# A hybrid trunk layer: triangular inverse on POOL, token shift without copies, key norms by logarithm, undecayed states, pooling beside the last group's fills through DRAM

## The chip, the cores and the metric

The kernel runs on one core of a Trainium2 chip. Its time is the device time of one execution in microseconds (us), as the median of several runs. All times below are from the kernel before the change unless a sentence says otherwise.

## What is computed

One layer of a streaming trunk for 256 prompt tokens and 64 sample tokens (320 together), with a model width of 2048, all in 32-bit floats:

```
h = RMSNorm(x);  [u_pool | u_rwkv | g_pool | g_rwkv] = h @ w_in
A: pooling mixer on u_pool: trailing means over 2/4/8/16 tokens minus the token, a linear map per group, a scale
B: RWKV-7 on u_rwkv: token shift, low-rank decay / rate / gate, 16 heads x 64,
   S = S * w_t + (S @ -kk) b_t + v_t k_t;  y = S @ r   (kk has norm 1), group norm, bonus
x += (sigmoid(g_pool) * (A @ proj_pool) + sigmoid(g_rwkv) * (B @ proj_rwkv)) @ w_out
x += SwiGLU(RMSNorm(x));  x += sigmoid(RMSNorm(x) @ w_ple_gate) * (p @ w_ple_proj);  final RMSNorm
```

Outputs are y and the new shift, pooling and wkv states.

## The kernel before

**Matmuls.** Every weight matrix streams from HBM in units of eight 128x128 blocks (`unit`): SP loads `raw`, ACT rounds it to `wh` (line 98), DVE takes the rest `wl = raw - wh` (`TT`, line 56), three buffers each. PE then does three matmuls of 320 columns per block (`mm3`, lines 115 to 117): `wh*xh`, `wh*xl`, `wl*xh`. A gemm with 16 blocks of depth has two units and 48 matmuls. The cast `wl_f0_8` is that of the fill tile f0 from block 8 on.

**The recurrence.** The 16 heads are worked on in four groups of four heads (`group`). A group takes six projected tiles (`acc_q...`), shifts them by one token (`shift`), and makes decay factors (`cum`, `p5`, `pcs`, `pinv`), the normalised keys (`rsqrt_tp`) and the operands `ar` and `bk` of five chunks of 64 tokens. Their products (PE, `g0` and `g4`) are masked on DVE into `mg`. Each 64x64 chunk matrix needs a triangular inverse. Its diagonal 32x32 blocks, 40 in a group, go through DRAM (`dF`, written and read by POOL's DMA queue) into a tile `xb` with one block on each of 40 partitions. 30 steps invert them there, each a multiplication into `tm` and an addition into `xb`, so 60 operations of 30 to 240 elements per partition. One `tensor_scalar` adds 1 on the diagonal; DMAs through `dX` and `dT` bring the blocks back, and PE makes the off-diagonal block (`pz`, `px`). Then four steps over the chunks (`ra`, `pu`, `ps_s`, `py_c`) carry the state `sbd`: new state = (`ps_s` + old state) times the decay `pcs`.

**Work between.** Behind group g stand `FILLS[g]` tiles of independent gemms (`acc_f`, 40 in all: 8 for `u_pool`, 32 for the gates), whose results go to DRAM. After the last group the pooling mixer (`pool_load`, `pool_diff`, `pool_mix`) reads `d_u` back, makes the differences on DVE, multiplies them by the pool weights (`acc_pw`), and the remaining five fills follow. Then come the projections, the feed-forward part and the last gate.

**Order.** A scheduler sets each engine's order from the program and its dependencies when the program is built; priorities (`tc.high_priority`) pull weight units ahead. Each engine runs its queue in order, and an instruction that waits holds back everything behind it. DVE and POOL have one such queue each; POOL's also issues its DMAs.

Of the kernel before, what the change touches and what calls it, by code (L numbers as in the profile page):

```python
# [48 lines left out]
def trunk_step(ctx: ExitStack, tc: tile.TileContext, xT, pT, cols, w_low, s0T, poolpast, cst, maskc, invc,  # L49
# [103 lines left out]
    def col(c, n=1):  # L153
        return ct[:, c:c + n]
# [3 lines left out]

    def shift(q, rp, t, out):

        pool.tensor_copy(out=rp[:, 0:5:4, 0], in_=ssz[:, q, :])
        pool.tensor_copy(out=rp[:, 1:4, 0], in_=rp[:, 0:3, C])
        pool.tensor_copy(out=nshift[:, q, :], in_=rp[:, 3:5, C])
        act.activation(t, rp[:, :, 1:], AF.Copy, scale=omu[:, q:q + 1])
        stt(out.rearrange("p (c t) -> p c t", c=NCH), rp[:, :, 0:C], col(C_MU + q), t, ALU.mult, ALU.add)


    fill_q = list(range(-8, 32))
# [20 lines left out]
    with tc.tile_pool(name="start", bufs=1) as st:  # L189
# [97 lines left out]
                        pe.matmul(out=acc[0:n], lhsT=w, rhs=x, start=k == 0 and n == P, stop=k == KD - 1 and n == P)  # L287

        def low(q, a=None):
            rp = st.tile([P, NCH, C + 1], F32, tag="rp", name="rp0", bufs=2)  # L290
            xs = xstd.rearrange("p (c t) -> p c t", c=NCH)
            if a is None:
                a = small(f"acc_t{q}", [P, NT], ("", "s", "cs")[q])
                if q == 2:
                    narrow(a, w_in[q])
                else:
                    gemm(a, w_in[q], KD, f"t{q}", xs_in)
            ac = a.rearrange("p (c t) -> p c t", c=NCH)
            if q == 2:
                r3 = st.tile([P, NT], F32, tag="xm0", name="r3", bufs=2)  # L300
                for i in range(3):
                    act.copy(r3[32 * i:32 * i + 32], a[96:128])
                TT(rp[0:96, :, 1:], ac[0:96], r3[0:96].rearrange("p (c t) -> p c t", c=NCH), ALU.add)
                mul(rp[0:96, :, 1:], rp[0:96, :, 1:], xs[0:96])
                mul(rp[96:128, :, 1:], ac[96:128], xs[96:128])
            else:
                mul(rp[:, :, 1:], ac, xs)
            t = st.tile([P, NCH, C], F32, tag="tsh", name="tsh0", bufs=2)
# [41 lines left out]
    def pool_diff(gi, z):  # L350

        pool.dma_start(out=o_pool[:, 0, 2 * gi:2 * gi + 2, :], in_=z[:, :, T_P:T_P + PAST])
        pool.dma_start(out=o_pool[:, 1, 2 * gi:2 * gi + 2, :], in_=z[:, :, ZL - PAST:])
        cur, w = z, 1
        while w < WINS[gi]:
            s = rf.tile([P, 2, ZL], F32, tag="tp", name="s", bufs=6)
            lo = 2 * w - 1
            TT(s[:, :, lo:], cur[:, :, lo:], cur[:, :, lo - w:ZL - w], ALU.add)
            cur, w = s, 2 * w
        d = rf.tile([P, 2, NT], F32, tag="tp", name="d", bufs=6)  # L360
        inv = 1.0 / WINS[gi]
        a, b = PAST, 2 * PAST + T_P
        t16 = rk.tile([P, 2, 16], F32, tag="tm", name="t16")
        mul(t16, cur[:, :, a:a + 16], iv[:, gi:gi + 1, :].broadcast_to([P, 2, 16]))
        TT(d[:, :, 0:16], t16, z[:, :, a:a + 16], ALU.subtract)
        stt(d[:, :, 16:T_P], cur[:, :, a + 16:a + T_P], inv, z[:, :, a + 16:a + T_P], ALU.mult, ALU.subtract)
        stt(d[:, :, T_P:], cur[:, :, b:], inv, z[:, :, b:], ALU.mult, ALU.subtract)
        dh = rf.tile([P, 2, NT], F32R, tag="tp", name="dh", bufs=6)
        act.copy(dh, d)
        dl = rf.tile([P, 2, NT], F32R, tag="tp", name="dl", bufs=6)  # L370
        TT(dl, d, f(dh), ALU.subtract)
        return dh, dl

    def pool_mix(gi, dh, dl):
        h, l = unit(w_poolw[gi], 4, f"pw{gi}")
        for i in range(2):
            j = 2 * gi + i
            a = small("acc_pw", [P, NT])
            mm3(a, [h[:, (2 * i + q) * P:(2 * i + q + 1) * P] for q in range(2)],
                [l[:, (2 * i + q) * P:(2 * i + q + 1) * P] for q in range(2)],  # L380
                [(dh[:, q, :], dl[:, q, :]) for q in range(2)], True, True)
            act.activation(yah[:, j, :], a, AF.Copy, scale=col(C_PS + j))
            stt(yal[j], a, col(C_PS + j), f(yah[:, j, :]), ALU.mult, ALU.subtract)

    def gate_tile(i):
        gt = sp.tile([P, NT], F32, tag="gate", name="gate", bufs=2)
# [6 lines left out]
    with tc.tile_pool(name="rk", bufs=1) as rk:  # L393

        def shift_tile(q, out):

            a = acc_tile(f"acc_q{q}")
            gemm(a, w_in[q], KD, f"q{q}", xs_in)
            rp = rf.tile([P, NCH, C + 1], F32, tag="rp", name="rp", bufs=3)
            mul(rp[:, :, 1:], a.rearrange("p (c t) -> p c t", c=NCH), xstd.rearrange("p (c t) -> p c t", c=NCH))  # L400
            t = rf.tile([P, NCH, C], F32, tag="tsh", name="tsh", bufs=2)
            shift(q, rp, t, out)

        W2 = [P, 2, NT]
# [1 line left out]
        def tp(name):  # L406
            return rf.tile(W2, F32, tag="tp", name=name, bufs=6)
# [15 lines left out]
        def group(g):  # L423
# [141 lines left out]
            for s in range(1, 31):  # L565
                n = 31 - s
                tm = rk.tile([40, s, n], F32, tag="tm", name="tm")
                mul(tm, xb[:, 0:s, s:s + 1].broadcast_to([40, s, n]), xb[:, s:s + 1, s + 1:32].broadcast_to([40, s, n]))
                TT(xb[:, 0:s, s + 1:32], xb[:, 0:s, s + 1:32], tm, ALU.add)
            diag = xb.rearrange("u s t -> u (s t)")[:, 0:1024:33]  # L570
            vec.tensor_scalar(out=diag, in0=diag, scalar1=1.0, scalar2=None, op0=ALU.add)
            act.copy(xbt, xb[0:20].rearrange("u s t -> u t s"))
# [30 lines left out]
            sbd_in = rk.tile([P, 2, P], F32, tag="sbd", name="sbd_in", bufs=4)  # L603
            pool.memset(sbd_in, 0.0)
            for h in range(2):
                pool.dma_start(out=sbd_in[64 * h:64 * h + 64, :, 64 * h:64 * h + 64],
# [11 lines left out]
                                  rhs=uv[:, c, 2 * jj + h, :], start=cur is None and h == 0, stop=h == 1)  # L618

            states = {4: sbd_in, 0: None}  # L620
            for cs in ((4, 0), (1,), (2,), (3,)):
                n = len(cs)
                ra = small("ra", [P, n, 2, C], "cs")
# [19 lines left out]
                                      rhs=uv[:, c, 2 * jj + h, :], start=True, stop=True)  # L643
                new = {}
                for i, c in enumerate(cs):
                    nxt = rk.tile([P, 2, P], F32, tag="sbd", name="sbd", bufs=4)
                    pool.memset(nxt, 0.0)
                    for lo in halves:
                        src = ps[lo, i]
# [65 lines left out]
        pool.dma_start(out=o_shift, in_=nshift)
        part = ap.tile([P, KD, NT], F32, tag="ah", name="part")
# [231 lines left out]
```

## Time and profile before

| | |
|---|---|
| median of 3 runs | 1900.65 us (1900.62 to 1900.97) |
| profiled execution | 1900.61 us, of which span 1898.7 us |
| busy: PE, DVE, ACT, POOL | 98%, 59%, 42%, 7% of the span |
| chain that ended last | PE 95%, DVE 3%, DMA 1%, issue 1% |
| mean granted TensorE clock | 0.993 |

The profiled execution is 1.9 us longer than its span, which runs from the first to the last instruction. In rows of the profile the engines are PE (matmul), DVE (vector), ACT (scalar), POOL (GpSimd) and SP (which issues weight loads); a row names its engine, its line of the kernel, its operation, `out<-in` by tile names, and the shape.

### The profile page before, as it was taken

To read this page: it belongs to the slowest core of one execution; us is meant where nothing else is said; L and a number is where in the kernel's file an instruction comes from. 1 tells how busy PE (TensorE), PEld (TensorE's weight loads), DVE (VectorE), ACT (ScalarE), POOL (GpSimd) and SP (SyncE) were. 2 spreads that over 40 slices of the span, in tenths; PEclk is the share of its full clock that TensorE was granted. 3 is DMA by queue.
4 is the path that set the end of the run, shared out by engine and by line. 5 is a ranking of instruction groups with operands and counts; after the bars stand their busy time and mean duration, and the time that the engine had idled before them with its cause. 6 is when DMAs were issued, how large, how long until landed. Compare 5 with 4: busy or idle time off the path is not lost.

```text
span 1898.7 us, 32757 instructions
## 1 busy us (share of the span) xinstructions
PE 1863.8 (98%) x13444; PEld 1838.0 (97%) x13444; DVE 1120.1 (59%) x1674; ACT 798.6 (42%) x1060; POOL 138.7 (7%) x282
## 2 busy tenths in 40 slices
PE   8999999899999999999999999999999999999997
PEld 7999999799989999999999999999999999999997
DVE  7676976877857465555454554444545554445655
ACT  6554536464455334443333333223333333333543
POOL 0110222202310112000000000000000000000000
PEclk9999999899999999999999999999999999999998
DMA  7554544345545657444444444554444444555553
GB/s 274 168 170 150 167 147 148 105 161 181 169 138 189 199 191 233 146 152 148 151 150 149 152 147 148 146 151 156 153 146 154 146 154 143 152 146 150 169 170 117
DMA packets 95349, 302.99 MB, mean 160 GB/s; under 512 B 12224, under 2 KB 23248, under 8 KB 95200
## 3 DMA queue, kind: packets, MB, share of 16 engines
q1 hardware_dynamic: 78336, 271.71, 44.3%
q0 software_dynamic: 6816, 17.39, 3.0%
q10 hardware_dynamic: 10048, 11.80, 1.7%
q8 instruction: 106, 1.74, 0.4%
q14 instruction: 43, 0.35, 0.1%
HBM read 284.12 MB, written 16.73 MB: 158 GB/s over the span
## 4 chain that ended last, share of the span: by engine, by line
PE 95%; DVE 3%; DMA 1%; issue 1%; ACT 0%; SPq 0%; DVEq 0%; ACTq 0%
PE acc_fd L115 5%; PE acc_fu L116 5%; PE acc_fg L116 5%; PE acc_fg L115 5%; PE acc_fg L117 5%; PE acc_fu L117 5%; PE acc_fd L116 5%; PE acc_fu L115 5%; PE acc_fd L117 5%; PE acc_f L115 4%; PE acc_f L116 4%; PE acc_f L117 4%; PE acc_q L117 3%; PE acc_q L115 3%; PE acc_q L116 3%; PE acc_pg L115 2%
## 5 line engine op out<-in xcount | busy, mean ns | idle before, releaser
L116 PE MATMUL acc_fg<-nl,wh_fg 128*128 128x320 f32 x704 | 217.8, 309 | 0.0
L115 PE MATMUL acc_fg<-nh,wh_fg 128*128 128x320 f32 x704 | 217.6, 309 | 0.1
L115 PE MATMUL acc_fu<-nh,wh_fu 128*128 128x320 f32 x704 | 217.5, 309 | 0.0
L117 PE MATMUL acc_fu<-nh,wl_fu 128*128 128x320 f32 x704 | 217.5, 309 | 0.0
L116 PE MATMUL acc_fu<-nl,wh_fu 128*128 128x320 f32 x704 | 217.5, 309 | 0.0
L117 PE MATMUL acc_fg<-nh,wl_fg 128*128 128x320 f32 x704 | 217.5, 309 | 0.0
L56 DVE TENSOR_TENSOR wl_fd<-raw_fd,wh_fd 128x1024 fp32r<-128x1024 f32 (+1 forms) x96 | 109.1, 1136 | 151.7 <-ACT wh_fd L98 151.7
L98 ACT CAST wh_fd<-raw_fd 128x1024 fp32r<-128x1024 f32 (+1 forms) x96 | 94.1, 980 | 203.1 <-PE acc_fd L116 162.4
L98 ACT CAST wh_fg<-raw_fg 128x1024 fp32r<-128x1024 f32 x88 | 92.5, 1051 | 199.1 <-PE acc_fg L116 98.7
L98 ACT CAST wh_fu<-raw_fu 128x1024 fp32r<-128x1024 f32 x88 | 92.5, 1052 | 190.8 <-PE acc_fu L116 103.4
L56 DVE TENSOR_TENSOR wl_fg<-raw_fg,wh_fg 128x1024 fp32r<-128x1024 f32 x88 | 107.8, 1225 | 105.3 <-ACT wh_fg L98 105.3
L115 PE MATMUL acc_f<-xh,wh_f 128*128 128x320 f32 x512 | 160.8, 314 | 1.7 <-ACT wh_f L98 1.7
L116 PE MATMUL acc_f<-xl,wh_f 128*128 128x320 f32 x512 | 160.6, 314 | 0.0
L117 PE MATMUL acc_f<-xh,wl_f 128*128 128x320 f32 x512 | 159.5, 312 | 0.8 <-DVE wl_f L56 0.8
L115 PE MATMUL acc_fd<-hh,wh_fd 128*128 128x320 f32 x512 | 158.2, 309 | 0.0
L116 PE MATMUL acc_fd<-hl,wh_fd 128*128 128x320 f32 x512 | 158.2, 309 | 0.0
L117 PE MATMUL acc_fd<-hh,wl_fd 128*128 128x320 f32 x512 | 158.2, 309 | 0.0
L56 DVE TENSOR_TENSOR wl_fu<-raw_fu,wh_fu 128x1024 fp32r<-128x1024 f32 x88 | 107.8, 1226 | 83.9 <-ACT wh_fu L98 83.9
L115 PEld LDWEIGHTS acc_fg<-nh,wh_fg 128*128 128x128 f32 x704 | 132.2, 188 | 0.3 <-issue 0.3
L116 PEld LDWEIGHTS acc_fg<-nl,wh_fg 128*128 128x128 f32 x704 | 132.2, 188 | 0.1
L117 PEld LDWEIGHTS acc_fg<-nh,wl_fg 128*128 128x128 f32 x704 | 132.2, 188 | 0.1
L116 PEld LDWEIGHTS acc_fu<-nl,wh_fu 128*128 128x128 f32 x704 | 132.2, 188 | 0.0
(490 smaller groups left out, 4913.0 us busy)
## 6 DMA issues: line engine op xcount, KB each, us to landing
raw_fg<-in_w_gate SPq DMA_DIRECT2D x88, 512.0 KB, 3.7
raw_fu<-in_w_up SPq DMA_DIRECT2D x88, 512.0 KB, 3.7
raw_f<-in_w_in SPq DMA_DIRECT2D x64, 512.0 KB, 4.0
raw_fd<-in_w_down SPq DMA_DIRECT2D x64, 512.0 KB, 3.6
raw_q<-in_w_in SPq DMA_DIRECT2D x48, 512.0 KB, 3.9
raw_o<-in_w_out SPq DMA_DIRECT2D x32, 512.0 KB, 3.7
raw_pg<-in_w_pg SPq DMA_DIRECT2D x32, 512.0 KB, 3.9
raw_fd<-in_w_down SPq DMA_DIRECT2D x32, 384.0 KB, 3.5
```

The lines of the kernel that those rows point to most:

```text
L56: return vec.tensor_tensor(out=out, in0=a, in1=b, op=op)
L98: act.copy(h, raw)
L115: pe.matmul(out=acc, lhsT=hs[i], rhs=xh, start=first and i == 0, stop=False)
L116: pe.matmul(out=acc, lhsT=hs[i], rhs=xl, start=False, stop=False)
L117: pe.matmul(out=acc, lhsT=ls[i], rhs=xh, start=False, stop=last and i == n - 1)
```

## The change

Five edits, and what follows from them:

1. The 60 operations of the inverse move from DVE to POOL. The diagonal operation stays on DVE.
2. `shift` keeps a tile without a spare column per chunk; the two POOL copies into it go, and DVE does the two first tokens in an operation of its own, 128x2.
3. `rsqrt_tp` takes the inverse of the root as exp(-ln) on ACT in place of DVE's reciprocal.
4. The state is handed on without its decay: `sbd` is the sum, the decay goes into a tile `dec` beside it, and POOL multiplies the decay into `ar` for the chunks that read it (`later`, 768 elements a partition).
5. The pooling mixer stands between group 3 and its fills, loads its weights on POOL's queue and writes to DRAM (`d_ya`); the result is read back behind the fills. All 40 fills now stand behind groups (`FILLS` ends in 27).

```diff
-FILLS = (5, 4, 4, 22)
+FILLS = (5, 4, 4, 27)
...
     def shift(q, rp, t, out):
-        pool.tensor_copy(out=rp[:, 0:5:4, 0], in_=ssz[:, q, :])
-        pool.tensor_copy(out=rp[:, 1:4, 0], in_=rp[:, 0:3, C])
-        pool.tensor_copy(out=nshift[:, q, :], in_=rp[:, 3:5, C])
-        act.activation(t, rp[:, :, 1:], AF.Copy, scale=omu[:, q:q + 1])
-        stt(out.rearrange("p (c t) -> p c t", c=NCH), rp[:, :, 0:C], col(C_MU + q), t, ALU.mult, ALU.add)
+        pool.tensor_copy(out=nshift[:, q, :], in_=rp[:, T_P - 1:NT:T_S])
+        act.activation(t, rp, AF.Copy, scale=omu[:, q:q + 1])
+        stt(out[:, 1:], rp[:, 0:NT - 1], col(C_MU + q), t[:, 1:], ALU.mult, ALU.add)
+        stt(out[:, 0:T_P + 1:T_P], ssz[:, q, :], col(C_MU + q), t[:, 0:T_P + 1:T_P], ALU.mult, ALU.add)
...
     def pool_mix(gi, dh, dl):
-        h, l = unit(w_poolw[gi], 4, f"pw{gi}")
+        raw = rf.tile([P, 4 * P], F32, tag="tp", name="raw_pw", bufs=6)
+        pool.dma_start(out=raw, in_=w_poolw[gi])
+        h = rf.tile([P, 4 * P], F32R, tag="tp", name="wh_pw", bufs=6)
+        act.copy(h, raw)
+        l = rf.tile([P, 4 * P], F32R, tag="tp", name="wl_pw", bufs=6)
+        TT(l, raw, f(h), ALU.subtract)
...
-            act.activation(yah[:, j, :], a, AF.Copy, scale=col(C_PS + j))
-            stt(yal[j], a, col(C_PS + j), f(yah[:, j, :]), ALU.mult, ALU.subtract)
+            o = sp.tile([P, NT], F32, tag="gate", name="pool_o", bufs=2)
+            act.activation(o, a, AF.Copy, scale=col(C_PS + j))
+            act.dma_start(out=d_ya[j], in_=o)
...
+            later = ar[:, :, 1:4].rearrange("p j c s t -> p j c (s t)")
+            pool.tensor_tensor(out=later, in0=later, in1=pcs[:, :, 0:3].unsqueeze(3).broadcast_to([P, 2, 3, P]),
+                               op=ALU.mult)
...
-                mul(tm, xb[:, 0:s, s:s + 1].broadcast_to([40, s, n]), xb[:, s:s + 1, s + 1:32].broadcast_to([40, s, n]))
-                TT(xb[:, 0:s, s + 1:32], xb[:, 0:s, s + 1:32], tm, ALU.add)
+                pool.tensor_tensor(out=tm, in0=xb[:, 0:s, s:s + 1].broadcast_to([40, s, n]),
+                                   in1=xb[:, s:s + 1, s + 1:32].broadcast_to([40, s, n]), op=ALU.mult)
+                pool.tensor_tensor(out=xb[:, 0:s, s + 1:32], in0=xb[:, 0:s, s + 1:32], in1=tm, op=ALU.add)
...
-                        if states[c] is not None:
-                            TT(nxt[lo, :, lo], src, states[c][lo, :, lo], ALU.add)
-                            src = nxt[lo, :, lo]
-                        mul(nxt[lo, :, lo], src, pcs[lo, :, c:c + 1].broadcast_to([64, 2, C]))
+                        if states[c] is None:
+                            vec.tensor_copy(out=new_s, in_=ps[lo, i])
+                        else:
+                            old = sbd_in[lo, :, lo] if c == 4 else dec[c][lo]
+                            TT(new_s, ps[lo, i], old, ALU.add)
...
+                    for lo, new_s in zip(halves, at):
+                        mul(dec[c + 1][lo], new_s, pcs[lo, :, c:c + 1].broadcast_to([64, 2, C]))
...
             act.activation(s, am, AF.Sqrt)
+            act.activation(s, s, AF.Ln)
             r = tp("r")
-            vec.reciprocal(out=r, in_=s)
+            act.activation(r, s, AF.Exp, scale=-1.0)
...
             group(g)
+            if g == 3:
+                for gi in range(4):
+                    pool_mix(gi, *pool_diff(gi, pool_load(gi)))
             fill(n)
...
-        for gi in range(4):
-            pool_mix(gi, *pool_diff(gi, pool_load(gi)))
+        for j in range(8):
+            yt = sp.tile([P, NT], F32, tag="gate", name="ya", bufs=2)
+            pool.dma_start(out=yt, in_=d_ya[j])
+            act.copy(yah[:, j, :], yt)
+            TT(yal[j], yt, f(yah[:, j, :]), ALU.subtract)
```

How the order of instructions moves is seen at three places. The first is POOL's queue at the inverse of group 0, before the change: token-shift copies and the DMAs around `xb`.

```order
L162 COPY rp<-rp 128x3
L163 COPY nshift<-rp 128x2
L561 DMA dF<-mg 32x20x32 x2
L564 DMA xb<-dF 40x1024
```

In the changed program the same place reads as follows (`ar` is the operand that `later` multiplies).

```order
L539 TENSOR_TENSOR ar<-ar,pcs 128x2x384
L569 DMA dF<-mg 32x20x32 x2
L161 COPY nshift<-rp 128x2
L572 DMA xb<-dF 40x1024
L161 COPY nshift<-rp 128x2
L576 TENSOR_TENSOR tm<-xb 40x30
L578 TENSOR_TENSOR xb<-xb,tm 40x30
L576 TENSOR_TENSOR tm<-xb 40x58
L578 TENSOR_TENSOR xb<-xb,tm 40x2x29
```

The 60 operations now stand behind the load of `xb` in POOL's queue, each waiting for the one before it; in the run of group 0 only three copies stand between them.

The second place is DVE's queue around the diagonal operation of group 0, before the change (names with their buffer numbers; `bk` is group 1's already).

```order
L56 TENSOR_TENSOR xb_1172<-xb_1172,tm_1252 40x27x4
L56 TENSOR_TENSOR wl_q18_0_3238<-raw_q18_0_3234,wh_q18_0_3236 128x1024
L62 SCALAR_TENSOR_TENSOR bk_2335<-kkr_2307,pinv_2305 128x10x64
L56 TENSOR_TENSOR tm_1255<-xb_1172 40x84
L571 TENSOR_SCALAR xb_1172<-xb_1172 40x32
L62 SCALAR_TENSOR_TENSOR xk_3024<-rp_3156,ct_85,tsh_3158 128x320
L56 TENSOR_TENSOR wl_q18_8_3268<-raw_q18_8_3264,wh_q18_8_3266 128x1024
```

In the changed program the diagonal operation has become line 580.

```order
L56 TENSOR_TENSOR wl_f-1_0_2895<-raw_f-1_0_2891,wh_f-1_0_2893 128x1024
L468 SCALAR_TENSOR_TENSOR cum_2288<-rmask_97,sig_2260 128x320 x2
L56 TENSOR_TENSOR ar_2324<-xr_1840,p5_2291 128x10x64
L56 TENSOR_TENSOR wl_f-1_8_2925<-raw_f-1_8_2921,wh_f-1_8_2923 128x1024
L56 TENSOR_TENSOR fill_o_2887<-acc_f-2_2826,xstd_92 128x320
L56 TENSOR_TENSOR wl_f0_0_2959<-raw_f0_0_2955,wh_f0_0_2957 128x1024
L56 TENSOR_TENSOR sp_l_2306<-sq_2299,sp_h_2304 128x640
L580 TENSOR_SCALAR xb_1166<-xb_1166 40x32
L56 TENSOR_TENSOR wl_f0_8_2989<-raw_f0_8_2985,wh_f0_8_2987 128x1024
L489 TENSOR_SCALAR am_2300<-s_kk_2308 128x640
```

The diagonal operation stands in DVE's queue at a fixed place between weight casts and waits there for the 54th of POOL's 60 operations (that of step 27); before, it waited for work of its own queue only.

The third place is POOL's queue in group 3 of the changed program, where the pooling mixer's loads stand (`raw_pw` is its weight, `z` its input).

```order
L700 DMA gs<-d_gs 128x2x320
L576 TENSOR_TENSOR tm<-xb 40x220
L578 TENSOR_TENSOR xb<-xb,tm 40x20x11
L374 DMA raw_pw<-in_w_poolw 128x512
L576 TENSOR_TENSOR tm<-xb 40x210
L578 TENSOR_TENSOR xb<-xb,tm 40x21x10
L576 TENSOR_TENSOR tm<-xb 40x198
L578 TENSOR_TENSOR xb<-xb,tm 40x22x9
L576 TENSOR_TENSOR tm<-xb 40x184
L341 MEMSET z 128x2x15
L342 DMA z<-in_poolpast 128x2x15
L344 DMA z<-d_u 128x2x256
```

Before, the weight was loaded on SP's queue and `z` after the last group; now the second scale's weight is issued behind 40 operations of the inverse, and the third scale's `z` behind 45.

## Rows read from the trace of the kernel before

**Rows 1.** The page: span, and the chain that ended last by engine.
```profile
span 1898.7 us, 32757 instructions
PE 95%; DVE 3%; DMA 1%; issue 1%; ACT 0%; SPq 0%; DVEq 0%; ACTq 0%
```
**Rows 2.** Windows of 5 us, 345 to 360 us; columns head the group.
```profile
core 0: us, PE busy (x) PEld busy (x) DVE busy (x) ACT busy (x) POOL busy (x), PEclk, DMA share, GB/s
...
345.00:350.00 5.00, 1.66 (x25) 1.15 (x26) 4.88 (x10) 2.66 (x5) 1.57 (x3) 0.95 0.80 250
350.00:355.00 5.00, 1.43 (x20) 1.24 (x20) 4.91 (x10) 0.83 (x2) 1.07 (x3) 0.50 0.35 118
355.00:360.00 5.00, 4.37 (x25) 4.28 (x26) 4.47 (x9) 1.99 (x4) 2.61 (x6) 0.53 0.00 0
```
**Rows 3.** Waits of PE, 320 to 364 us: total us, times, longest.
```profile
PE ra L613 <- DVE sbd L56: 6.4, 2, 4.2
PE pu L633 <- ACT rhs L627: 0.7, 1, 0.7
PE ps_s L642 <- ACT uv L636: 0.5, 1, 0.5
```
**Rows 4.** Timeline of DVE, 336 to 362 us: start, duration, operation.
```profile
337.49 4.15 DVE L697 RECIPROCAL r<-s 128x640 f32<-128x640 f32 x1 [2.14 <-ACT s L695]
```
**Rows 5.** One window, 555 to 585 us; columns as in rows 2.
```profile
555.00:585.00 30.00, 24.30 (x210) 21.50 (x209) 25.16 (x53) 15.07 (x26) 4.91 (x8) 0.94 0.38 123
```
**Rows 6.** The inverse's operations on DVE by tile: min/median/max ns.
```profile
L56 DVE TENSOR_TENSOR tm<-xb x120: 182/338/401, 166.5 to 506.1; 40x30 f32<-40x30 f32 x8, 40x58 f32<-40x58 f32 x8, 40x84 f32<-40x84 f32 x8, 40x108 f32<-40x108 f32 x8
L56 DVE TENSOR_TENSOR xb<-xb,tm x120: 175/338/402, 167.1 to 506.8; 40x30 f32<-40x30 f32 x8, 40x58 f32<-40x58 f32 x8, 40x84 f32<-40x84 f32 x8, 40x108 f32<-40x108 f32 x8
```
**Rows 7.** Groups of ACT's instructions: busy us, mean ns.
```profile
L695 ACT ACT_TABLE_LOAD x4 | 5.1, 1283 | 2.9 <-DVE am L485 2.9
```
**Rows 8.** Timeline of POOL near 65, 148 and 219 us.
```profile
65.72 1.14 POOL L161 COPY rp<-ssz 128x2 f32<-128x2 f32 x1
147.78 0.19 POOL L162 COPY rp<-rp 128x3 f32<-128x3 f32 x1 [6.75 <-DVE rp L56]
148.02 0.19 POOL L161 COPY rp<-ssz 128x2 f32<-128x2 f32 x1
219.47 3.94 POOL L161 COPY rp<-ssz 128x2 f32<-128x2 f32 x1
```
**Rows 9.** Timeline of DVE at the same places; last two first and last of six.
```profile
65.59 1.23 DVE L56 TENSOR_TENSOR wl_q<-raw_q,wh_q 128x1024 fp32r<-128x1024 f32 x1 [0.44 <-ACT wh_q L98]
147.23 0.48 DVE L56 TENSOR_TENSOR rp<-acc_q,xstd 128x320 f32<-128x320 f32 x1
148.13 1.23 DVE L56 TENSOR_TENSOR wl_q<-raw_q,wh_q 128x1024 fp32r<-128x1024 f32 x1 [0.42 <-ACT wh_q L98]
219.16 1.20 DVE L56 TENSOR_TENSOR wl_q<-raw_q,wh_q 128x1024 fp32r<-128x1024 f32 x1
...
222.15 1.21 DVE L56 TENSOR_TENSOR wl_q<-raw_q,wh_q 128x1024 fp32r<-128x1024 f32 x1
```
**Rows 10.** Groups of POOL's memsets: busy us, mean ns.
```profile
L647 POOL MEMSET sbd<- 128x256 f32 x20 | 6.2, 315 | 67.2 <-DVE sbd L56 37.5 <-PE acc_q L117 12.8 <-PE py_c L617 9.0
L542 POOL MEMSET uv<- 64x1280 f32 x4 | 4.7, 1165 | 6.2 <-PE py_c L617 3.6 <-PE acc_q L117 2.5
```
**Rows 11.** Timeline of PE, 157 to 161 us: first and last of 28 gemm matmuls.
```profile
157.00 0.31 PE L115 MATMUL acc_q<-xh,wh_q 128*128 128x320 f32 x1
...
160.95 0.31 PE L115 MATMUL acc_q<-xh,wh_q 128*128 128x320 f32 x1
```
**Rows 12.** Timelines of PE and DVE around group 0's last products.
```profile
155.95 0.72 PE L515 MATMUL g<-ar,bk 64*128 64x128 f32 x8
...
166.49 0.18 DVE L56 TENSOR_TENSOR tm<-xb 40x30 f32<-40x30 f32 x1
```
**Rows 13.** Groups of DVE's instructions, 40 to 560 us: busy us, mean ns.
```profile
L56 DVE TENSOR_TENSOR wl_f<-raw_f,wh_f 128x1024 fp32r<-128x1024 f32 x54 | 65.6, 1215 | 14.3 <-ACT wh_f L98 14.2
L464 DVE TENSOR_TENSOR_SCAN cum<-rmask,sig 128x320 f32<-128x320 f32 x8 | 6.1, 804 | 0.0
L62 DVE SCALAR_TENSOR_TENSOR xr<-rp,ct,tsh 128x320 f32<-128x320 f32 x8 | 4.4, 552 | 0.3 <-POOL rp L162 0.2
```

More of the change, by code (lines that the diff above doesn't have):

```diff
@@ L289, in low @@
         def low(q, a=None):
-            rp = st.tile([P, NCH, C + 1], F32, tag="rp", name="rp0", bufs=2)
-            xs = xstd.rearrange("p (c t) -> p c t", c=NCH)
+            rp = st.tile([P, NT], F32, tag="rp", name="rp0", bufs=2)
             if a is None:
@@ L297, in low @@
                     gemm(a, w_in[q], KD, f"t{q}", xs_in)
-            ac = a.rearrange("p (c t) -> p c t", c=NCH)
             if q == 2:
@@ L302, in low @@
                     act.copy(r3[32 * i:32 * i + 32], a[96:128])
-                TT(rp[0:96, :, 1:], ac[0:96], r3[0:96].rearrange("p (c t) -> p c t", c=NCH), ALU.add)
-                mul(rp[0:96, :, 1:], rp[0:96, :, 1:], xs[0:96])
-                mul(rp[96:128, :, 1:], ac[96:128], xs[96:128])
-            else:
-                mul(rp[:, :, 1:], ac, xs)
-            t = st.tile([P, NCH, C], F32, tag="tsh", name="tsh0", bufs=2)
+                TT(rp[0:96], a[0:96], r3[0:96], ALU.add)
+                mul(rp[0:96], rp[0:96], xstd[0:96])
+                mul(rp[96:128], a[96:128], xstd[96:128])
+            else:
+                mul(rp, a, xstd)
+            t = st.tile([P, NT], F32, tag="tsh", name="tsh0", bufs=2)
             out = st.tile([P, NT], F32, tag="xm0", name="xm0", bufs=2)
@@ L336, in trunk_step @@
         TT(t2s[64:96], t2[64:96], f(t2s[64:96]), ALU.subtract)
+    d_ya = dr.tile([8, P, NT], F32, name="d_ya")
     ZL = PAST + T_P + PAST + T_S
@@ L362, in pool_diff @@
         a, b = PAST, 2 * PAST + T_P
-        t16 = rk.tile([P, 2, 16], F32, tag="tm", name="t16")
+        t16 = rk.tile([P, 2, 16], F32, tag="t16", name="t16")
         mul(t16, cur[:, :, a:a + 16], iv[:, gi:gi + 1, :].broadcast_to([P, 2, 16]))
@@ L398, in shift_tile @@
             gemm(a, w_in[q], KD, f"q{q}", xs_in)
-            rp = rf.tile([P, NCH, C + 1], F32, tag="rp", name="rp", bufs=3)
-            mul(rp[:, :, 1:], a.rearrange("p (c t) -> p c t", c=NCH), xstd.rearrange("p (c t) -> p c t", c=NCH))
-            t = rf.tile([P, NCH, C], F32, tag="tsh", name="tsh", bufs=2)
+            rp = rf.tile([P, NT], F32, tag="rp", name="rp", bufs=3)
+            mul(rp, a, xstd)
+            t = rf.tile([P, NT], F32, tag="tsh", name="tsh", bufs=2)
             shift(q, rp, t, out)
@@ L602, in group @@
             ysb = rk.tile([P, NCH, 2, C], F32, tag="ysb", name="ysb")
-            sbd_in = rk.tile([P, 2, P], F32, tag="sbd", name="sbd_in", bufs=4)
+            sbd_in = rk.tile([P, 2, P], F32, tag="sbd", name="sbd_in", bufs=3)
             pool.memset(sbd_in, 0.0)
@@ L620, in group @@
             states = {4: sbd_in, 0: None}
+            dec = {}
             for cs in ((4, 0), (1,), (2,), (3,)):
@@ L645, in group @@
                 for i, c in enumerate(cs):
[L646 to L649, printed above, removed]
-                        if states[c] is not None:
-                            TT(nxt[lo, :, lo], src, states[c][lo, :, lo], ALU.add)
-                            src = nxt[lo, :, lo]
-                        mul(nxt[lo, :, lo], src, pcs[lo, :, c:c + 1].broadcast_to([64, 2, C]))
+                    dec[c + 1] = rk.tile([P, 2, C], F32, tag="dec", name="dec", bufs=3)
+                    if c < 3:
+                        nxt = rk.tile([P, 2, P], F32, tag="sbd", name="sbd", bufs=3)
+                        pool.memset(nxt, 0.0)
+                        at = [nxt[lo, :, lo] for lo in halves]
+                    else:
+                        nxt = None
+                        at = [dec[c + 1][lo] for lo in halves]
+                    for lo, new_s in zip(halves, at):
+                        if states[c] is None:
+                            vec.tensor_copy(out=new_s, in_=ps[lo, i])
+                        else:
+                            old = sbd_in[lo, :, lo] if c == 4 else dec[c][lo]
+                            TT(new_s, ps[lo, i], old, ALU.add)
                     new[c] = nxt
+                    for lo, new_s in zip(halves, at):
+                        mul(dec[c + 1][lo], new_s, pcs[lo, :, c:c + 1].broadcast_to([64, 2, C]))
                     if c >= 3:
+                        d = dec[c + 1]
                         for h, lo in enumerate(halves):
                             pool.dma_start(out=o_wkv[c - 3, 4 * g + h:4 * g + 4:2].rearrange("j k v -> k j v"),
-                                           in_=nxt[lo, :, lo])
+                                           in_=d[lo])
                 py = wide("py_c", tag="cw")[:, 0, 0:n * P].rearrange("p (i h v) -> p i h v", i=n, h=2)
```

## The prediction

> **What bounds the kernel now.** I read the page first. TensorE (PE) holds 95% of the chain that ended last and DVE 3%, in a span of 1898.7 us [rows 1]. PE's own work is the same before and after, so only the places where PE stands idle or at a low clock can be won, and the reader should look for those in the windows. Outside the first 42 us and the tail, which the change leaves alone, there are two. The first is at 345 to 360 us: in three windows of 5 us PE is busy 1.66, 1.43 and 4.37 us at a granted clock of 0.95, 0.50 and 0.53 [rows 2]. That is 1.58 + 0.72 + 2.32 = 4.6 us of full-speed work in 15, so 10.4 us lost, while DVE is busy over 4.4 us in each. The waits of the stretch name what was late: 6.4 us for sbd from DVE, 0.7 and 0.5 us for ACT, 7.6 us in all [rows 3]. [...] DVE was late because a reciprocal of 4.15 us stood in front of the casts and states [rows 4]. The second place is 555 to 585 us, where the pooling mixer runs after the fills are used up: PE is busy 24.30 of 30 us at 0.94, so 30 - 22.8 = 7.2 us are lost [rows 5].
>
> **What the change takes away.** DVE loses the 60 small operations of the inverse per group; each half of them takes 338 ns at the median [rows 6]. It loses the reciprocal and one of two state operations per chunk step. The first stall then has no cause left: I count 10.4 us. The pooling mixer moves to between group 3 and 27 matmul fills, which cover its chain: 7.2 us. Its result goes to DRAM and comes back in eight POOL loads while the fills run; PE wants it only after the last fill, so I cost it at nothing; without the fills in front it would be the old 7.2 us. Ten more table loads on ACT at 1.28 us [rows 7] are hidden, since ACT has 0% of the chain [rows 1]; if each stood on the path, they would cost 13 us. The extra 128x2 operation of the token shift on DVE is small, and two POOL copies per tile go. Possible gain: 17.6 us.
>
> **What it adds: 240 dependent operations on POOL.** No POOL arithmetic of this kind is in the trace, so I bound one. A 128x2 copy without neighbours takes 0.19 us, and POOL starts it 0.07 us after the end of the DVE operation it waited for [rows 8, 9]; call 0.25 us the part without data. Memsets of 256 and 1280 elements take 315 and 1165 ns [rows 10], so a stream costs POOL 0.83 ns an element. The first 54 operations of a group hold 9576 elements, 177 each. Multiply and add read two streams and write one. If all three overlap it is 0.25 + 0.15 = 0.40 us each; if the two reads take turns, 0.55 us; if all three take turns, 0.70 us. I take 0.55, the middle. As one group's 54 operations: 21.5, 29.6 or 37.7 us.
>
> [...]
>
> **POOL also has to share with DVE.** Copies of two elements show it. At 65.72 us one takes 1.14 us instead of 0.19; a weight cast, which reads two SBUF tiles, ran from 65.59 to 66.82 and the copy ended with it [rows 8, 9]. At 219.47 a copy takes 3.94 us: DVE had operations with two SBUF inputs back to back from 219.16 to 223.36 and POOL did not get in between [rows 8, 9]. A copy that began 0.1 us before a cast was not stretched, and the cast began 0.11 us into it (148.02 and 148.13) [rows 8, 9]. So what POOL reads waits for the whole of a DVE operation with two SBUF inputs, and I add these up, less 0.1 us each.
>
> **Where it ends on PE.** After group 0's 54th inverse operation comes the diagonal operation, which stays on DVE and waits for it. Behind it in DVE's queue stands the cast wl_f0_8, which PE needs for the second half of fill 0. In the changed order PE has 315 gemm matmuls and 34 smaller ones between the last g product and that cast's first use. The gemms follow each other every (160.95 - 157.00) / 27 = 0.146 us [rows 11]; 20 of the smaller are as wide, the others come to some 0.1 us (eight matmul records of products took 0.72 [rows 12]). That makes 50.5 us. Off this come 9.8 us from the product's end to the first inverse operation (156.67 to 166.49, through the mask, two DMA hops and their waits [rows 12]), and 0.2 + 1.2 us for diagonal and cast. POOL has 39.3 us. The new multiplication `later` runs beside the mask operation and adds nothing unless it exceeds 2 us.
> - Group 0 needs 29.6 us of its own, plus DVE's operations with two SBUF inputs from the first inverse operation to the diagonal: nine casts at 1.215, four token shifts at 0.55, two scans at 0.80 [rows 13], and the low-rank casts, two 640-wide operations and small ones for 4.0, which makes 18.7 us; plus three copies (0.6), less 20 times 0.1. That is 46.9, so 7.6 us late.
> - Group 1: 317 gemm and 69 small matmuls, 54.2 us, of which POOL has 43.0. DVE's share is 20.8 (group norm comes in), and memsets, copies and DMA issues stand in the run, of which I count half, 2.5 us: 50.9, so 7.9 late.
> - Group 2: 312 and 63, 52.9 us, POOL has 41.7; it needs 51.1: 9.4 late.
> - Group 3: here the first thing late is a pooling weight load on POOL behind 40 inverse operations, which PE wants 49.5 us after the last product. Less 9.8 and some 4 us for transfer and split POOL has 35.7; it needs 21.9 + 16.5 + 4 - 2 = 40.4: 4.7 late.
>
> Together 29.6 us of waiting, times 1.37 is 40.5. **Sum:** 40.5 - 17.6 = +23, on the profiled execution's 1900.61 (the median is 1900.65): **1923 us**. With 0.40 us per operation POOL is late by 1 us in group 2 alone: 1885. With 0.70 the waits grow by 30 us: 1965.
>
> **Rivals.** (1) POOL is in time: the operations take under about 0.47 us, or DVE and POOL get in each other's way less in a stream than single copies show. 0.08 us times 54, 54, 54 and 40 operations is 16 us of the 29.6, and the 13 that are left, times 1.37, equal the gain; that is the point from which it decides. Then both stalls go and the time is 1883 to 1895. For it: a copy that is ahead of a cast is not stretched. Against: the ten-fold and twenty-fold copies. Chance of faster: 0.28. (2) The gain and the new waits cancel, 1897 to 1904: 0.06. [...] I give it 0.2 of the 0.66 for slower. (4) The edits to DVE do nothing, because the first stall has another cause: 1933. DVE busy 4.9 of 5 us there [rows 2] speaks against it; it lies inside the slower case.
>
> Changes under 0.2% (3.8 us) this measurement can't tell from none. The range reaches from 1882 (all of the gain and a little) to 1955; given that it is slower, I expect 1908 to 1950.
>
> **What would show it.** In the changed profile: POOL's inverse operations of 40x240 at 0.4 to 0.8 us alone and over 1 us beside a weight cast; PE waiting for wl_f from DVE in groups 0 to 2, and DVE in turn for POOL before the diagonal operation; windows with a clock near 0.5 behind these waits; no wait for sbd at group 2 and no hole after the last fill; and a first inverse operation some 10 us after the last product. The prediction is wrong if a group's inverse on POOL ends within 40 us of its start while DVE casts, or if the stall at 345 us stays.

## The result, and the profile of the changed kernel

The changed kernel takes 1923.65 us (median of 4 runs, 1921.14 to 1924.83), the kernel before 1900.63 us beside it; the ratio is 1.0121 with a 95% interval of 1.0104 to 1.0139. It is slower, by 23 us. The profiled execution has a span of 1923.0 us, 24.3 more than before.

The page, its span and the chain that ended last, against [rows 1]:

```profile
span 1923.0 us, 32768 instructions
PE 80%; POOL 10%; DMA 3%; issue 3%; DVE 3%; ACT 1%; SPq 0%; ACTq 0%; DVEq 0%; POOLq 0%
```

POOL was not in the chain before and now holds 10% of it, and PE's share falls from 95% to 80%.

Windows of the changed kernel (columns as in [rows 2]): four stretches behind the four inverses, and the two old holes.

```profile
205.00:235.00 30.00, 23.18 (x166) 21.70 (x166) 15.69 (x21) 18.74 (x21) 12.03 (x24) 0.72 0.38 115
310.00:330.00 20.00, 15.74 (x90) 15.14 (x88) 7.90 (x10) 12.57 (x15) 9.84 (x18) 0.83 0.47 137
415.00:445.00 30.00, 24.06 (x193) 23.30 (x192) 14.52 (x18) 21.05 (x25) 13.19 (x24) 0.83 0.41 122
500.00:530.00 30.00, 26.56 (x170) 25.91 (x170) 21.84 (x28) 15.58 (x22) 26.92 (x33) 0.94 0.59 182
340.00:365.00 25.00, 24.47 (x258) 21.86 (x257) 20.89 (x34) 8.54 (x17) 5.97 (x10) 1.00 0.35 111
555.00:585.00 30.00, 29.90 (x320) 28.00 (x319) 18.85 (x36) 15.67 (x31) 4.51 (x9) 1.00 0.59 189
```

Both old holes [rows 2, 5] are closed: 340 to 365 us loses 0.5 us and 555 to 585 us 0.1. Length less busy time times clock gives what the new stretches lose: 30 - 23.18 x 0.72 = 13.3 us, then 6.9, 10.0 and 5.0 us, 35.2 us in all. A part of it is the clock, which at times stood at its lower level there (0.50) behind PE's idle time; two windows of 5 us in the first stretch show it:

```profile
210.00:215.00 5.00, 3.67 (x14) 3.67 (x15) 2.41 (x4) 2.06 (x2) 3.07 (x7) 0.50 0.45 143
225.00:230.00 5.00, 5.00 (x55) 4.61 (x54) 4.97 (x9) 4.43 (x6) 0.00 (x0) 0.50 0.34 111
```

The waits of PE in group 0's stretch, 200 to 240 us (total us, times, longest), name two late engines:

```profile
PE acc_f L117 <- DVE wl_f L56: 3.8, 1, 3.8
PE acc_q L115 <- ACT wh_q L98: 2.3, 1, 2.3
PE acc_q L117 <- DVE wl_q L56: 0.6, 1, 0.6
```

In the other three stretches the largest waits are these, one in group 1 (300 to 350 us), one in group 2 (405 to 450) and two in group 3 (495 to 560):

```profile
PE s_kk L421 <- ACT sp_h L415: 4.0, 1, 4.0
PE acc_f L117 <- DVE wl_f L56: 4.7, 1, 4.7
PE acc_pw L115 <- ACT pool_o L386: 2.0, 1, 2.0
PE acc_pw L115 <- ACT wh_pw L376: 2.0, 2, 1.4
```

And the waits of DVE and of ACT from 160 to 240 us say what those two waited for themselves:

```profile
DVE xb L580 <- POOL xb L578: 9.3, 1, 9.3
...
ACT xb L581 <- POOL xb L578: 12.4, 1, 12.4
```

DVE stood for 9.3 us at the diagonal operation, with the weight cast behind it. ACT stood for 12.4 us at the copy that transposes the inverse (line 581), with its own half of the next casts behind it. In group 1 one of these is `sp_h`, for which PE waited 4.0 us: the cast starts at 319.95 us, behind that copy, which starts at 316.45.

The timeline of POOL shows the price of an operation: three multiplications and two additions that no DVE operation stretched, and in the last row an addition beside a weight cast; the rows of DVE below belong to it:

```profile
212.30 0.25 POOL L576 TENSOR_TENSOR tm<-xb 40x30 f32<-40x30 f32 x1
205.58 0.51 POOL L576 TENSOR_TENSOR tm<-xb 40x168 f32<-40x168 f32 x1
188.54 0.61 POOL L576 TENSOR_TENSOR tm<-xb 40x240 f32<-40x240 f32 x1
212.63 0.26 POOL L578 TENSOR_TENSOR xb<-xb,tm 40x30 f32<-40x30 f32 x1
187.81 0.65 POOL L578 TENSOR_TENSOR xb<-xb,tm 40x238 f32<-40x238 f32 x1
189.23 1.56 POOL L578 TENSOR_TENSOR xb<-xb,tm 40x240 f32<-40x240 f32 x1
```

```profile
188.85 1.38 DVE L56 TENSOR_TENSOR wl_f-1_0_2895<-raw_f-1_0_2891,wh_f-1_0_2893 128x1024 fp32r<-128x1024 f32 x1 [0.49 <-ACT wh_f-1_0_2893 L98]
190.16 2.41 DVE L468 TENSOR_TENSOR_SCAN cum<-rmask,sig 128x320 f32<-128x320 f32 x2
199.16 1.31 DVE L56 TENSOR_TENSOR sp_l<-sq,sp_h 128x640 fp32r<-128x640 f32 x1
209.82 0.19 DVE L580 TENSOR_SCALAR xb<-xb 40x32 f32<-40x32 f32 x1 [9.35 <-POOL xb L578]
```

From 30 to 240 elements a multiplication grows from 0.25 to 0.61 us, so it costs 0.20 us and 1.71 ns an element; an addition grows from 0.26 to 0.65 us at 238 elements, 1.9 ns each. The next operation starts 0.08 us after the end of the one before (188.54 + 0.61 to 189.23). The operation at 189.23 met a weight cast and took 1.56 us. The DVE rows show the other direction too: two scans took 2.41 us in place of 1.6 [rows 13], the 640-wide subtraction 1.31 us in place of 0.81 in the kernel before; DVE waits for POOL as POOL waits for DVE.

### The profile page after: what moved, and what is told of

Same layout as the page of the kernel before. It is cut to its first block, busy times and chain, and to the rows that moved or that the text cites. A ratio compares the mean times of both kernels' runs of the same rounds, so it can differ in the third digit from the quotient of the medians.

```text
span 1923.0 us, 32768 instructions
## 1 busy us (share of the span) xinstructions
PE 1874.6 (97%) x13444; PEld 1847.7 (96%) x13444; DVE 1073.3 (56%) x1465; ACT 817.7 (43%) x1086; POOL 294.8 (15%) x476
## 4 chain that ended last, share of the span: by engine, by line
PE 80%; POOL 10%; DMA 3%; issue 3%; DVE 3%; ACT 1%; SPq 0%; ACTq 0%; DVEq 0%; POOLq 0%
PE acc_fd L115 5%; PE acc_fu L116 5%; PE acc_fg L115 5%; PE acc_fg L116 5%; PE acc_fg L117 5%; PE acc_fu L117 5%; PE acc_fu L115 5%; PE acc_fd L117 5%; PE acc_fd L116 5%; POOL tm L576 4%; POOL xb L578 4%; PE acc_q L117 2%; PE acc_q L115 2%; PE acc_q L116 2%; PE acc_pg L115 2%
## 5 line engine op out<-in xcount | busy, mean ns | idle before, releaser
L854 POOL DMA_DIRECT2D pp<-d_pp x16 | 8.6, 540 | 1117.5 <-DVE gt L56 1117.5
L117 PE MATMUL acc_f<-xh,wl_f 128*128 128x320 f32 x512 | 163.6, 320 | 8.8 <-DVE wl_f L56 8.8
```

The source lines that it names most:

```text
L117: pe.matmul(out=acc, lhsT=ls[i], rhs=xh, start=False, stop=last and i == n - 1)
L854: pool.dma_start(out=pp, in_=d_pp[m])
```

## Experiments

**The inverse back on DVE, all other edits kept.**

```diff
-                pool.tensor_tensor(out=tm, in0=xb[:, 0:s, s:s + 1].broadcast_to([40, s, n]),
...
-                pool.tensor_tensor(out=xb[:, 0:s, s + 1:32], in0=xb[:, 0:s, s + 1:32], in1=tm, op=ALU.add)
+                mul(tm, xb[:, 0:s, s:s + 1].broadcast_to([40, s, n]), xb[:, s:s + 1, s + 1:32].broadcast_to([40, s, n]))
+                TT(xb[:, 0:s, s + 1:32], xb[:, 0:s, s + 1:32], tm, ALU.add)
```

> The changed kernel with the 60 inverse operations of each group back on DVE and all else as changed. Theory A (the inverse on POOL is late, the other edits gain): the waits for wl_f and wh_q behind the inverse go, the stall at 345 us stays away, 1883 to 1892 us. Rival B (the other edits cost the time: the ten more table loads on ACT, the pooling loads and the read-back on POOL): 1912 us or more.

Measured: 1911.67 us, ratio 1.0059 (1.0044 to 1.0074). That is 12 us less than the changed kernel and 11 us more than before: theory A's number is missed by 20 us and the time stands at rival B's bound. The gain that I had booked for the other edits does not come in this order. Its trace puts the largest single loss at one of the places that rival B named, the read-back of the pooling result. With the inverse in DVE's queue the scheduler places the pooling mixer later, and the last fills are over before the eight loads are. Windows of 5 us of this kernel:

```profile
610.00:615.00 5.00, 2.71 (x12) 1.60 (x10) 4.73 (x10) 3.47 (x7) 0.54 (x1) 0.87 0.54 167
615.00:620.00 5.00, 4.26 (x16) 4.27 (x17) 2.62 (x5) 1.14 (x3) 1.08 (x2) 0.50 0.89 271
620.00:625.00 5.00, 3.31 (x13) 1.98 (x11) 1.79 (x4) 1.86 (x5) 1.03 (x2) 0.84 0.54 192
625.00:630.00 5.00, 4.59 (x20) 3.79 (x20) 1.89 (x4) 2.18 (x4) 1.66 (x4) 0.77 0.30 87
```

20 us hold 2.36 + 2.13 + 2.78 + 3.53 = 10.8 us of full-speed work, so 9.2 us are lost where the changed kernel loses none, of 22 us that windows of 5 us add up to between 60 and 640 us (17.6 in the kernel before); the first load is issued at 600.93 us and the last at 624.50, against 570.78 and 593.47 in the changed kernel. A wait of 4.2 us for `tzz` (the inverse's way back) in group 0 is the next largest; with the low clock behind it, 235 to 250 us loses 7 us.

**The inverse moved to POOL, all other edits left out** (the same lines, in the kernel before).

> The kernel before with nothing changed but the 60 inverse operations of each group on POOL. Theory A: PE starves in all four groups as in the changed kernel, and the hole of the pooling mixer after the last group stays: 1925 to 1940 us. Rival B: DVE is relieved and the stall at 345 us goes, 1888 to 1902 us.

Measured: 1931.11 us, 1.0163 (1.0146 to 1.0180), as theory A had it. The 54 operations of a group take 42.3, 47.2, 45.6 and 45.9 us from the first one's start. Two windows of this kernel:

```profile
340.00:365.00 25.00, 25.00 (x267) 22.99 (x265) 20.39 (x35) 11.19 (x20) 11.14 (x16) 1.00 0.40 127
570.00:615.00 45.00, 35.51 (x286) 31.81 (x285) 29.38 (x60) 18.41 (x32) 4.92 (x8) 0.92 0.33 102
```

The stall at 345 us is gone though the reciprocal is still there: relieving DVE of the inverse ends it, so the changed kernel gets that gain from the move and needs no logarithm for it. PE comes there some 18 us later in this run, after its waits in groups 0 and 1, which also gives DVE time. But with only six steps moved (the third kernel of the table below) some 5 us are lost ahead of it, the reciprocal stands, and the stall is gone too:

```profile
340.00:365.00 25.00, 25.00 (x234) 22.91 (x233) 19.97 (x34) 9.69 (x17) 7.96 (x17) 1.00 0.43 139
```

The hole of the pooling mixer stays (45 - 35.51 x 0.92 = 12.3 us lost). All other edits together are worth 7.5 us on top of the moved inverse, less than that hole.

**Nobody waits for the inverse in DVE's and ACT's queues.**

```diff
-            vec.tensor_scalar(out=diag, in0=diag, scalar1=1.0, scalar2=None, op0=ALU.add)
-            act.copy(xbt, xb[0:20].rearrange("u s t -> u t s"))
+            pool.tensor_scalar(out=diag, in0=diag, scalar1=1.0, scalar2=None, op0=ALU.add)
+            pool.tensor_copy(out=xbt, in_=xb[0:20].rearrange("u s t -> u t s"))
```

> The changed kernel with the diagonal operation and the transposing copy of the inverse on POOL too, so that neither DVE nor ACT stands waiting for the inverse with weight casts behind. Theory A (the inverse itself comes too late, whoever waits): PE waits at pz instead, since its order is fixed, 1908 to 1925 us. Rival C (only the two waiting instructions in DVE's and ACT's queues starve PE): 1885 to 1898 us.

Measured: 1920.09 us, 1.0105 (1.0090 to 1.0120). PE's waits from 200 to 560 us in this kernel:

```profile
PE pz L596 <- DMA tzz<-dT: 16.0, 3, 7.3
PE acc_pw L115 <- ACT wh_pw L376: 3.9, 1, 3.9
PE acc_q L117 <- DVE wl_q L56: 2.1, 1, 2.1
```

The wait for wl_f is all but gone (0.3 us in place of 8.8) and that for wh_q is gone; those for wl_q (2.1) and wh_pw (3.9) are left, and `pz` takes the place of the others. But this run does more than free the two queues: on POOL the copy takes 2.45 us in group 0, against 1.99 on ACT, and the way back starts behind it. From the end of the 54th operation to the issue of the load of `tzz` it is 13.3, 12.8 and 10.2 us in groups 0 to 2, against 9.7, 9.9 and 10.7 in the changed kernel, so some 6.6 of the 16.0 us at `pz` are this run's own. The other 9 us are waiting for the inverse itself. Taking the 6.6 us off, at 1.58 us of time for each (the factor of the changed kernel, worked out below), gives an estimate of 1910 us, still above rival C's range: the two waiters alone do not explain the loss. That their place in the queues costs nothing is not shown.

**Sharing between DVE and POOL**, with an extra DVE operation of two SBUF inputs, and with one of a single input, behind eight weight casts of the changed kernel. The extra operations are work that nobody uses.

```diff
             TT(l, raw, f(h), ALU.subtract)
+            if name in EXTRA:
+                TT(raw, raw, f(h), ALU.subtract)
```

> The changed kernel with one more DVE subtraction of 128x1024 with two SBUF inputs behind the weight cast of each of eight units (fills -3 to 0), whose result nobody uses; seven fall beside group 0's inverse. Theory A (POOL waits out each such DVE operation): group 0's inverse up to the diagonal takes 48 to 51 us where it took 42.7, and the kernel 1929 to 1937 us. Rival D (POOL's own length sets it and DVE beside it costs little): 42 to 44 us and 1921 to 1926 us.

```diff
             TT(l, raw, f(h), ALU.subtract)
+            if name in EXTRA:
+                vec.tensor_reduce(out=spare, in_=raw, axis=AX.X, op=ALU.add)
```

> The same as the run with a second subtraction, but the extra DVE operation is a sum over the 1024 elements of the raw tile: as long, with one SBUF input. Theory A: POOL does not wait for it, group 0's inverse takes 42 to 44 us, the kernel 1921 to 1926 us. Rival E (any busy DVE slows POOL): as long as with the second subtraction.

Measured: 1931.20 us, 1.0167 (1.0152 to 1.0182), with the subtraction, and 1920.91 us, 1.0111 (1.0096 to 1.0126), with the sum, a tenth of a microsecond below the range that I gave for it. The timelines of POOL and DVE in the run with the subtraction, the first inverse operation and the diagonal:

```profile
166.29 0.67 POOL L579 TENSOR_TENSOR tm<-xb 40x30 f32<-40x30 f32 x1 [0.81 <-DMA xb<-dF]
214.90 0.19 DVE L583 TENSOR_SCALAR xb<-xb 40x32 f32<-40x32 f32 x1 [13.52 <-POOL xb L581]
```

The same with the sum, whose operations take as long, 1.22 us:

```profile
173.48 1.22 DVE L103 TENSOR_REDUCE spare<-raw_f-3_8_2795 128x1 f32<-128x1024 f32 x1 [0.60 <-DMA raw_f-3_8_2795<-in_w_in]
...
165.16 0.23 POOL L580 TENSOR_TENSOR tm<-xb 40x30 f32<-40x30 f32 x1
208.51 0.19 DVE L584 TENSOR_SCALAR xb<-xb 40x32 f32<-40x32 f32 x1 [7.32 <-POOL xb L582]
```

From the first operation to the diagonal it is 48.6 us against 43.3, and 42.7 in the changed kernel. PE's wait for wl_f grows to 10.2 us, against 3.0. Six extra subtractions stand ahead of the diagonal in the order of that kernel (I had counted seven), so each cost POOL some 0.9 us of the 1.2 that it takes alone. All eight sums stand ahead of it in the other kernel and cost 0.7 us together. Rivals D and E fall.

**The key norms alone**, in the kernel before.

```diff
             act.activation(s, am, AF.Sqrt)
+            act.activation(s, s, AF.Ln)
             r = tp("r")
-            vec.reciprocal(out=r, in_=s)
+            act.activation(r, s, AF.Exp, scale=-1.0)
```

> The kernel before with nothing changed but the key norms: Ln and Exp on ACT in place of DVE's reciprocal. Theory A (the reciprocal in front of the casts made the stall at 345 us): the stall goes, 1887 to 1893 us. Rival B (two more table loads per group at 1.28 us hold the weight casts on ACT): 1897 to 1905 us.

Measured: 1900.55 us, 1.0003 (0.9993 to 1.0012): no change, a number inside rival B's range, but not for rival B's reason. Two windows of this kernel:

```profile
340.00:365.00 25.00, 23.92 (x215) 22.05 (x215) 22.82 (x37) 10.09 (x16) 6.26 (x17) 1.00 0.46 152
450.00:500.00 50.00, 46.41 (x463) 43.45 (x463) 33.47 (x76) 16.07 (x29) 6.02 (x12) 0.93 0.42 133
```

The old stall is down to 1.1 us, as theory A had it; but between 450 and 500 us, where the kernel before had PE busy for 49.98 of 50 us, 6.8 us are lost, with one wait of 3.6 us for `tzz`, the way back of group 2's inverse. The kernel before there, and the places of the last products (`g`) and of `pz` in PE's timeline, first before and then in this run:

```profile
450.00:500.00 50.00, 49.98 (x502) 47.20 (x501) 36.65 (x85) 19.91 (x30) 9.44 (x17) 1.00 0.48 148
```

```profile
459.09 0.72 PE L515 MATMUL g<-ar,bk 64*128 64x128 f32 x8
465.21 0.82 PE L587 MATMUL pz<-tzz,mg 32*32 32x32 f32 x40
...
450.19 0.72 PE L515 MATMUL g<-ar,bk 64*128 64x128 f32 x8
457.04 1.19 PE L587 MATMUL pz<-tzz,mg 32*32 32x32 f32 x40 [3.59 <-DMA tzz<-dT]
```

The inverse is no later on DVE: its last load is issued 1.3 us after these products in the kernel before (461.12 us) and 0.3 us after them here (451.19). But PE now comes to `pz` 2.5 us after them (457.04 less the wait), where it came 5.4 us after them before; the scheduler has put `pz` ahead of `pb`. Most of the gain is given back there, and 2.9 us more at 235 to 245 us, behind a second wait for `tzz` of 1.4 us.

**The pooling mixer back behind the fills, with the inverse on DVE.**

```diff
-FILLS = (5, 4, 4, 27)
+FILLS = (5, 4, 4, 22)
...
-            if g == 3:
-                for gi in range(4):
-                    pool_mix(gi, *pool_diff(gi, pool_load(gi)))
             fill(n)
...
-        for j in range(8):
-            yt = sp.tile([P, NT], F32, tag="gate", name="ya", bufs=2)
-            pool.dma_start(out=yt, in_=d_ya[j])
...
+        for gi in range(4):
+            pool_mix(gi, *pool_diff(gi, pool_load(gi)))
```

> As the run with the inverse on DVE, with the pooling mixer back at its old place behind the fills (22 fills in the last group, weights on SP's queue, no way through DRAM). Theory A: the 12.7 us that run lost between 600 and 640 us waiting for the read-back go, the old hole of 7 to 10 us after the fills comes back: 1902 to 1909 us. Rival B (the table loads and the other edits cost the time, not the place of the pooling): 1910 us or more.

Measured: 1904.41 us, 1.0023 (1.0014 to 1.0033), as theory A had it: 7 us less than with the pooling moved (the read-back had cost 9.2 us and not the 12.7 that I had put down). So in that order the pooling edit loses, since no fills are left to cover the read-back.

**The reciprocal back in the changed kernel** (the key-norm lines turned round).

> The changed kernel with DVE's reciprocal back in the key norms in place of Ln and Exp. Theory F (after the late inverse ACT has Sqrt, Ln and Exp with three table loads, 6.0 us, between two weight casts, and PE waits for the second cast): the waits for wh_q in group 0 and for sp_h and s_kk in group 1 shrink, 1914 to 1921 us. Rival G (the loads are hidden and the reciprocal of 4.15 us costs DVE more): 1924 us or more.

Measured: 1918.66 us, 1.0101 (1.0085 to 1.0117). The time fits theory F, but its interval overlaps the changed kernel's, and the waits do not carry it: in group 0 the 2.3 us for wh_q become 2.3 us for wl_q, and the 4.0 us for sp_h in group 1 stay. Whether the table loads cost anything stays open.

**Part of the inverse on POOL.** Twelve of 30 steps, then six, in the changed kernel; six in the kernel before; and twelve with the reciprocal and the pooling as before, so that of the change only that, the token shift and the undecayed state are left.

```diff
-                pool.tensor_tensor(out=tm, in0=xb[:, 0:s, s:s + 1].broadcast_to([40, s, n]),
...
+                eng = pool if s <= 12 else vec
+                eng.tensor_tensor(out=tm, in0=xb[:, 0:s, s:s + 1].broadcast_to([40, s, n]),
...
```

> The changed kernel with the first 12 of the 30 inverse steps on POOL and the other 18 on DVE. POOL then has 24 operations of a group in place of 60, some 13 us alone. Theory A: the inverse is in time in every group, 1883 to 1893 us. Rival B: 1912 us or more.

> The changed kernel with only the first 6 of the 30 inverse steps on POOL (12 operations, some 5 us alone) and 24 steps on DVE. Theory A: POOL is in time and DVE has room, so the inverse costs PE nothing; with the pooling covered by the fills, 1883 to 1893 us. Rival H (DVE, with most of the inverse back, is late again, and the read-back of the pooling comes late as with the whole inverse on DVE): 1898 to 1910 us.

> The kernel before with the first 6 of the 30 inverse steps on POOL and nothing else changed. Theory A: DVE loses some 3 us of work per group, enough to end the stall at 345 us, the hole of the pooling mixer stays: 1888 to 1896 us. Rival: it moves to another wait, as in the run with the logarithm alone: 1897 to 1903 us.

> The changed kernel with 12 of 30 inverse steps on POOL, the reciprocal on DVE and the pooling mixer behind the fills as before; what is left of the change is the token shift without copies and the undecayed state. Theory A: no stall but the pooling mixer's hole of 7 to 10 us is left, 1886 to 1894 us. Rival: the state and shift edits bring nothing and small waits take its place, 1897 us or more.

| kernel | us | ratio (95%) |
|---|---|---|
| changed, 12 steps on POOL | 1899.35 | 0.9997 (0.9987 to 1.0006) |
| changed, 6 steps on POOL | 1893.46 | 0.9963 (0.9950 to 0.9976) |
| before, 6 steps on POOL | 1897.20 | 0.9983 (0.9973 to 0.9993) |
| 12 steps on POOL, reciprocal, pooling behind the fills | 1892.33 | 0.9957 (0.9942 to 0.9972) |

The first misses both ranges: its inverses are in time but for one wait of 1.3 us, but small waits on DVE and ACT (3.1 us for `mg`, 4.5 for `sp_h`) add up between 300 and 500 us. The second misses theory A's range by half a microsecond; the third lies on the edge of its rival's; the fourth is as theory A had it. Two of them beat both kernels, by 7 and 8 us on the kernel before; the third's 3 us lie under the 3.8 that I had taken as the least difference. The first and the fourth differ in the pooling edit and the key norms alone, and undoing both there is worth 7 us. What the token shift and the undecayed state bring by themselves no run isolates. Windows of the one with six steps:

```profile
205.00:235.00 30.00, 29.54 (x329) 28.07 (x327) 21.91 (x38) 22.04 (x30) 8.15 (x10) 1.00 0.49 151
340.00:365.00 25.00, 22.92 (x216) 20.64 (x215) 15.38 (x26) 7.75 (x13) 8.48 (x15) 1.00 0.40 126
555.00:585.00 30.00, 29.17 (x247) 27.46 (x246) 15.93 (x31) 15.03 (x31) 5.31 (x10) 1.00 0.65 208
```

Windows of the fourth:

```profile
340.00:365.00 25.00, 25.00 (x242) 22.55 (x241) 19.07 (x39) 8.97 (x16) 8.11 (x13) 1.00 0.47 135
555.00:585.00 30.00, 25.27 (x200) 23.02 (x195) 25.66 (x52) 15.04 (x23) 4.94 (x8) 1.00 0.46 132
```

The one covers the pooling mixer and keeps 2.1 us of small waits at 340; the other has no stall there and keeps the mixer's hole, 4.7 us in this window.

## Why the prediction was right

The forecast was 1923 us and slower; measured were 1923.65. By its steps:

- **Price of an operation on POOL.** Taken as 0.25 us and 1.7 ns an element with both reads in turn; measured 0.28 us (0.20 and the 0.08 to the next) and 1.71 ns for a multiplication, 1.9 for an addition. The 54 operations come to some 15 + 17 = 32 us alone, against 29.6 (29.4 by the rows' 0.83 ns). The `later` multiplication of 768 elements took 1.47 us ahead of the DMA, as assumed, and cost nothing.
- **Sharing with DVE.** Shown by the pair with the extra operations: up to the diagonal group 0's inverse took 48.6 us with those of two SBUF inputs and 43.3 with those of one, against 42.7 without any. But I over-counted it. Group 0's 54 operations took 42.7 us where I had 46.9; less 32 and 0.4 for two token-shift copies in the run (I had three), sharing cost some 10 us and not 16.7. Groups 1 and 2 took 47.5 and 45.6 us against 50.9 and 51.1.
- **Time POOL has.** From the last product's end (155.92 + 0.71) to the first operation, 167.13, it was 10.5 us against 9.8. PE came to the first use of wl_f0_8 50.9 us after the product (211.33 less the wait of 3.83), against 50.5.
- **Who waits.** The diagonal on DVE held the cast wl_f0_8, as said; I had missed that ACT's transposing copy waits for all 60 operations and holds casts as well, so that in group 1 PE waited for `sp_h` from ACT and hardly for wl_f (0.3 us), which I had named for groups 0 to 2. The run without either waiter shows that most of the waiting is for the inverse itself.
- **Waiting of PE.** 6.7, 5.2, 6.0 and 4.4 us in the four groups' stretches, 22.3 in all, where I had 7.6, 7.9, 9.4 and 4.7, together 29.6. The factor was 35.2 / 22.3 = 1.58 and not 1.37, which was the 10.4 us lost over the 7.6 us of waits in the first stall of the kernel before. The two errors work against each other: 35.2 us lost against 40.5. In group 3 it was the pooling chain, as said, though half of it at `pool_o`, which I had not named.
- **Gain.** 9.9 us at 340 and 7.1 at 555, 17.0 in all, against 17.6. The sum of these windows is +18.2 us, and the span grew by 24.3. Windows of 5 us from 60 to 640 us add up to 40.9 us lost, against 17.6 before, 23.3 more: some 5 us of that are waits of 0.2 to 1.3 us outside these stretches, which my sum did not have. So the total is as good as exact by some luck: the waits were too large in my sum, their factor and the rest too small.
- **What I had wrong of the causes.** I gave the first stall to the reciprocal and counted its end as a gain of all the DVE edits. The inverse alone on POOL ends it with the reciprocal in place, and the logarithm alone ends it too but brings nothing, since the wait comes back at group 2's `tzz`. And the other edits without the moved inverse are no 17.6 us faster but 11 us slower, in the order that the scheduler then finds. In group 0 ACT spent 6.0 us on three table loads and three activations between two weight casts; that this was hidden is neither shown nor refuted.

## What to carry to other kernels

A chain of small dependent operations moved from a half-idle DVE to POOL was late here by its own length plus what it shares with DVE (in group 0 some 32 us alone and 10 by sharing, with 39.3 us estimated for it): price it by elements, add the DVE operations with two SBUF inputs that stand beside it, and hold the sum against the time to the first thing that waits. An instruction that waits on another engine in the queue that also feeds PE held everything behind it (9.3 us on DVE and 12.4 on ACT in group 0), but with the chain itself late, moving it left much of the wait standing elsewhere (16.0 us at `pz`, some 9 of them for the inverse). Where a chain is too long for one engine, split it: with six of 30 steps on POOL the changed kernel gained 7 us on the kernel before, where with all 30 it lost 23. And a gain seen in one order of instructions is not a property of the edit: the logarithm ended a stall and gave it back 100 us later.

## What the runs showed of the hardware

POOL's tensor_tensor on 40 partitions cost 0.20 us and 1.7 ns (multiplication) to 1.9 ns (addition) an element, twice the 0.83 ns of its memsets [rows 10], also for slices of short rows and broadcast inputs; 128 partitions with 768 elements took 1.47 us, about the same rate. An extra DVE operation with two SBUF inputs cost POOL some 0.9 us of its 1.2, and eight with one input 0.7 us together, while the two-element copies of the kernel before had waited out the whole of it, 1.14 and 3.94 us in place of 0.19 [rows 8, 9]; that a part of each longer operation runs beside DVE's was not tried by itself. And DVE paid as well: its scans stretched from 0.80 to 1.2 us beside POOL's operations.
